# An attention kernel: GpSimd's parts of a product are released one VectorE instruction earlier, and the written order of the work is replaced

## The chip, the cores and the metric

The kernel runs on one core of a Trainium2 chip. The metric is the device time of one execution in microseconds (us); less is better. Times below are medians of several runs, and one execution was taken by the profiler as well.

## What is computed

Grouped-query attention over 8 batches, 8 query heads, 2 key/value heads, 1024 positions and a head size of 64, in float32 in and out:

```
for g in range(n_kv_heads):
    scores = scale * np.matmul(q_group, k_group.transpose(0, 1, 3, 2))
    attn = np.exp(scores - scores_max)
    attn = attn / (np.sum(attn, axis=-1, keepdims=True) + 1e-08)
    output[:, q_start:q_end, :, :] = np.matmul(attn, v_group)
```

## The kernel before

There are 64 jobs, one for each batch and query head. A job has 8 tiles of scores: 128 keys by 1024 queries, in PSUM. So 512 tiles of scores go through the kernel, and each needs an exponential before TensorE can multiply it with the values.

**TensorE** makes a tile with two matmuls (line 760), into one of three PSUM slots `sp`. Later it multiplies the exponentials with the values, 128 queries ("a piece") at a time, into the banks `ops` (line 824). A column of ones in `va` gives the sums of the softmax.

**ScalarE** turns most tiles into exponentials: one activation of 128x1024 from PSUM into `pt` (line 770).

**VectorE** does the rest by arithmetic on the bits of bfloat16, in steps:

- the pass (line 782): a tile from PSUM, scaled and shifted, written as 16-bit integers into `yt`. Two tiles share one buffer, and are called a chain;
- `zh` (line 790): the mantissa bits of `yt` as a number, into `zt`, over 2048 columns, SBUF to SBUF;
- `two` (line 797): the exponent bits of `yt`, into `et`, likewise;
- `mul` (line 806): `zt` times `yt`, SBUF and SBUF to SBUF.

The exponential is the sum of `et` and `zt`. TensorE forms the sum for nothing but more matmuls: it multiplies both with the values. Only the last three jobs add them on VectorE (`add`, line 811). When seven pieces are complete in a bank, VectorE takes the reciprocals of the sums (`rec`, line 889) and scales the outputs (`norm`, line 899), which SyncE's queue stores.

**GpSimd** takes a share of `mul`. The pass, `rec` and `norm` read PSUM; `zh`, `two` and `mul` read and write SBUF alone, and are called SBUF steps here. While VectorE is at a pass (and a `norm` or `rec` beside it), a window opens, and GpSimd multiplies a part of the columns of a chain whose `zh` is done and whose `mul` is still to come (line 738). VectorE's own `mul` is shorter by as much. GpSimd also issues the casting loads of q, k and v (line 518), and a small memset `tick` (line 733) which waits until the buffer of a new chain is free.

**The order** is written out by hand as a string `ORDER`, a letter for each step of TensorE and VectorE: `A` and `a` to `d` make a tile of scores for ScalarE or VectorE, `V` is a few matmuls with values, `W` waits, `p` or `P` is a pass, `r` or `R` a `rec`, `n` a `norm`, a digit is the next SBUF step of one of the open chains. The class `Plan` runs through it with a table of durations (the constants `M_...`, in ns) and makes a list of events with times. The kernel then issues the events by time, and every engine keeps that order. Nothing is decided on the chip.

GpSimd's parts come out of the plan. The function `Plan.gpsimd` is called at a pass, or at the `rec` ahead of it, with the length of the window. It lets a part begin `M_GLEAD` = 160 ns after VectorE has come to the window (or after GpSimd is free), counts `M_GFIX` = 190 ns and `M_GCOL` = 1.88 ns for each column, lets the part end `M_GOVER` = 60 ns behind the window, and makes it as wide as that allows, in steps of 8 columns. VectorE's next SBUF step is counted as held up from the point at which GpSimd ends over `M_GFREE` = 85 ns behind that step's start.

In the kernel, the part is made to wait for the VectorE instruction ahead of its window (`vec`, the last one issued):

```
tc.add_manual_dep(gps.ins, vec.ins.name, Sync, reason="VectorE needs the port before")
```

Of the kernel before, what the change touches and what calls it, by code (L numbers as in the profile page):

```python
# [30 lines left out]
M_D2 = 0.521  # L31
M_D4 = 0.261
M_REC = 115
M_GLEAD = 160
M_GFIX = 190
M_GCOL = 1.88
M_GOVER = 60
M_GLATE = 900
M_GFREE = 85
M_ISSUE = 850  # L40
M_OVER = 5000
NEED = 5150
M_GFREE = 85
M_OVER = 5000
NEED = 5150
M_NORM = 531
# [8 lines left out]
LONG = 6  # L55
GFROM = 2
GTO = 5
GMIN = 96
GREST = 64
GSTEP = 8  # L60
STEPS = (("zh", M_D4), ("two", M_D4), ("mul", M_D2), ("add", M_D2))


ORDER = """
AaApFFFFWWWWFAWWWWWWWWWWWWWWWWWWWWWWWWWWWWaWWWWWWWWWWApEEWWAW0WWWbWWWWApEEWWAW0WWWaWWWWApEEWWA0WWbFF
WAFFpFEAWWW0WWWAAE0W0WWWWWWWWWWWWWWWaRAnWWWWRWWWPWAVVVVVVVVnA0bWWWWApVVVVVVVVA0aWVpAVVVVVAR0bVVA0VVV
pVVVAVVVVnVAb0VVVApVVVAV0VVVVA0bVVRVPVAVVVVVAnbV0AVpVVVVVAVV0VVA0bVVRVPVAVVVVVAnbW0WWAVVpVVVVVVAV0VV
VVA0bWWRWAPVVVVVVVVAnbW0WWAVVpVVVVAVVV0VVVVA0cWWWRWAPVVVVVVVVAnbW0WWAVVVpVVVAVVV0VVVVAR0cWWWAPVVVVVV
VVAnbWW0WWAVVVpVVVVVAVV0VAc0VVVRVPAVVVVAnVA0WbVVVpVVVVAVVV0WVVA0bWWWWARPVVVVVVVVAncWWWA0VVVpVVVAVVVV
0VVA0bVVArPVVVVVVA0WcWWWAPVVVVVVVVAnAV0VVVV0VVVARb0VVVVPVVVAVVVVcnAVpVVVVVAVV0VVAb0VVVVRVAPVVVVVVAnW  # L70
cWWWA0VVVVpVVVVAVVV1VVAc0VARVPVVVVVVAWnWWWbA0VVVVVpVAVVVVVV0VAc0WWWAVpVVVVVVVA0WbWWARVPVVVVVVVAnWWcW
WA1VVVV0VVApVVVVVVVARWnWbWWApVVVVVVVVA0WcWWWApVVVVVVVVVA1cWWWARPVVVVVVVVVVAncWW1WAVVV2VVVVApVVVVVVVV
VA00WcWWAVVRVPVVVVVAVVnVVVA1bWWWWApVVVVVVVVA0cWWRWAPVVVVVVVVAncWW01WWAVVpVVVVVVAWV0VcA1VVVVpVAVVVVAR
0AVVc1VVVPVVVAVVVVnVAc1WWWWAVpVVVVVVVARWW0WcWWAPVVVVVVVVVAnWAV1VVVVVVVV1VcARVPVVVVVVAVnVVVA0cV1VVVVA
pVVVVVAW1WWWcWApVVVVVVVVA0cWWWARVPVVVVVVVAnWWcWWA1VVVVpVVVVAVVVVR0VAc1WWWAVPVVVVVVVAnWWcWA0VVVVVpVVV
AVVVVRV0Ac1WWWAVPVVVVVVVAWnWWWcA0VVVVVpVVVAVVVV2AAV0VVVVVV0VbWWARPVVVVVVVVVVAncWWWA1VVVVpVVVVVAVVVVr
V2VAc2WWWAVPVVVVVVVAnWWWbWA0VpVVVVVVVARWW2WcWWAVPVVVVVVVAnWWbWWA0VVVVpVVVVAVVV0VVAAWWRWWc0VVVVPVVVVA
VVVnVAA1VVVVV1VVVVVA0bVVVVRVPVVVVAVVVVAnc1VVVApVVVVVVVVA1WWbWWApVVVVVVVVVVAR0c1WWWAVVPVVVVVVAVVnVVVV
VA0bVVVpAVVVVVAR1bWWWWAPVVVVVVVVAncWW0WWAVVpVVVVVVAVV0VA1bVRVPVVAVVVVVnAA0VVVVV1VVVVVA0bVVpVAVVVVVVR
A1AVnVVVV1VbWWAipVVVVVVVVA0cWWWARPVVVVVVVVVAnbWWWA1VVVVpVVVVVAVVVV0cA0VVVVApVVVVVVVAR1AVVVnVVVVb1WWA  # L80
VpVVVVVVVVA0WcWAVpVVVVVVVVAR0AWWWbVV0VVVVAPVVVVVVVAncWWARPVVVVVVVAnWWAV1VVVVVV0cWAVpVVVVVVVA1WAWWcRV
nVVVVVpVVAVVVA01cVVpVAVVVVVV0AAWWW0WcVVVRVPVVVVAVVVnVVA1cWWWApVVVVVVVVA1AWWWbR0VVVVPVVVVAVVVnVVA1cWW
WApVVVVVVVVAR0WcWWWAPVVVVVVVVAnAV1VVVVVb0WAVpVVVVVVVARW0WcWWAPVVVVVVVVAnbWWWA1VVV0VVVVVApVVVVVVA0WcW
ARVPVVVVVVVVAnWAV1VVVVVVb0WWAVpVVVVVVVVVARW0WbWWAPVVVVVVVVVVAnAV1VVVVVVb0WAVpVVVVVVVVVARW0WAWWb0VVVV
VVPVVAVVVVVVVnVAb1WWAVpVVVVVVVA0WWbWARVPVVVVVVVAnWWAV1VVVVVV0VVVA1bVVVpVVAVVVVA0WbVRVPVVVAVVVVVAnA1W
VVVVVV1VVcAipVVVVVVVVA0WWbVRAPVVVVVAnVVA1bVV1VVVVApVVVVVVA0WbWWARPVVVVVVVVAnAV1VVVVVb1WAVpVVVVVVVARW
0WaWWAPVVVVVVVVAnbWWWW1WAVVVpVVVVVAVV0VVVA0aWWARPVVVVVVVVVAnAV1VVVVVVVb1AVpVVVVVVVVVARWW0WbWAPVVVVVV
VAVnVVVVVV1VAb1WWWWAVpVVVVVVVVVA0WWbWARVPVVVVVVVVAnWWbWWA1VVVVVpVVVVAVVV1bAVpVVVVAVV0VAr1cVVPVVAVVVV
AnAV1VVVVV0VVbARVpVVVVVVAWnWWWcWA1VVVVVpVVVAVVV0VVA0bWWWApVVVVVVVVAR1AWWWc1VVVVVPVVVAVVVVnVAb0WWWAVp
VVVVVVVARW1WAWWcV1VVVVVPVVAVVVVVnAc0WWWAVpVVVVVVVARWW1WbWAVPVVVVVVVAnWWcWA0VVVVpVVVAVVVV0cAVRpVVAVVV  # L90
VVnVAb1WWWWApVVVVVVVVA0cWWWRWAPVVVVVVVVAnbWW1WWAVVVpVVVVVAVV0VVVARc0WWWAPVVVVVVVVAnbWW1WAVVVpVVVVVVA
VV0VVAA0VVVV1VVVVVVVRc0AVPVVVVVVVAVnVVVA0bVVVApVVVVVVVVAR1AVVVnVVVVVV0VVVVA1aVVVpVAVVVVVVA0bWWWWARPV
VVVVVVVAnbWWW1WAVVV1VVVApVVVVVVVA0WbWWARPVVVVVVVVAnbWWW1WAVVVpVVVVVAVV1VAA0VVV0VVVVVVVVVVARnbVVVVpVA
VVVVVA0b0VVApVVVVVVVVAR0bWWWWAPVVVVVVVVVAnbW0WWAVVpVVVVVVAV0VVAARnVVVVV0VVVVVVVVA1AVVV1VVVVVV0VAAVVV
RVV0VVVVVVVVAnAVVV0VVVVVVVVVVVVVVRAnaWWWApVVVVVVVVVxVA0ArVnVVVVVVV0VA0AVVV0VVVVVLLRnLLLLLWWLFFRFn
"""


# [29 lines left out]
class Plan:  # L128
# [5 lines left out]
    def __init__(self, nj, npt, nct, nyt):  # L134
# [23 lines left out]
        s.tG, s.tB = M_START + 9000, 0  # L158
        s.due = [(NEED * j - 24000, "q", j) for j in [*range(10, nj, 2), nj - 1]]
        for b in range(1, 8):  # L160
            s.due.append((NEED * 8 * b - 16000, "v", (b, 0)))
            if b > 1:
                s.due.append((NEED * 8 * b - 25000, "k", (b, 0)))
        s.due.sort(key=lambda e: e[0])
# [42 lines left out]
    def gpsimd(self, s, t, window):  # L207


        while s.due:  # L210
            x = max(s.tG, s.due[0][0])
            if x + M_ISSUE > t + M_GLEAD:
                if t - s.due[0][0] <= M_OVER:
                    break
                x = max(t, s.tG)
            s.ev.append((x, s.due[0][1], None, s.due[0][2], None))
            s.tG = x + M_ISSUE
            s.due.pop(0)
        at = max(t, s.tG)
        until = t + window + M_GOVER  # L220
        at += M_GLEAD
        for ch in s.chains:
            if not (ch.zend <= at and 1 <= ch.at <= 2 and ch.nsteps == 3):
                continue
            if not GFROM <= ch.pairs[0][0] < self.nj - GTO:
                continue
            w = int((until - at - M_GFIX) / M_GCOL) // GSTEP * GSTEP
            if w < GMIN:
                break
            if ch.cols - w < GREST:  # L230
                w = ch.cols
            if not w:
                continue
            ch.cols -= w
            ch.wins += 1
            s.ev.append((t, "gmul", None, ch.id, (ch.cols, w)))
            s.tB = s.tG = at = at + M_GFIX + w * M_GCOL
            ch.parts += 1
            self.part(s, ch, s.tG + M_SEE + M_GLATE)

    def dve(self, s):
# [60 lines left out]
        else:  # L302
# [7 lines left out]
            if cols:  # L310
                s.ev.append((t, kind, None, ch.id, n, cols))
                end = at + M_FIX + cols * rate
                end += max(0, s.tB - at - M_GFREE)
            if kind == "zh":
# [123 lines left out]
def kernel(  # L438
# [13 lines left out]
    Sync = mybir.DependencyInfo(mybir.DependencyClass.Sync, mybir.DependencyReason.DATA)  # L452
# [216 lines left out]
    for j in range(NJ):  # L669
        b, h = divmod(j, H)  # L670
        at = need[j]
# [28 lines left out]
    def flat(t):  # L700
        return t.bitcast(BF16).rearrange("p i a b -> p (i a b)")
# [10 lines left out]
            elif (j, c) in pt:  # L712
                yield ci, pt[(j, c)][:, par, :]

    vec, gps = None, None
    turns, begun, ended, jobs = [], {}, {}, {}

    def begin(kind, j, gate):
# [4 lines left out]
    for when, kind, x, j, c, *cols in ev:  # L723
# [5 lines left out]
        elif kind == "gmul":  # L729
            lo, w = c  # L730
# [7 lines left out]
            begun[j] = gps = nc.gpsimd.tensor_tensor(  # L738
                out=z, in0=flat(yt[j])[:, lo : lo + w], in1=z, op=ALU.mult
            )  # L740
            tc.add_manual_dep(gps.ins, vec.ins.name, Sync, reason="VectorE needs the port before")
        elif kind == "tk":
            turn_k(*j)
        elif kind == "fv":
# [7 lines left out]
        elif kind == "score":  # L752
            b, h = divmod(j, H)
            t = kt[(b, h // HPG)]
# [21 lines left out]
        elif kind == "dpass":  # L776
            ch, i = j
            where[c] = j
            jobs.setdefault(ch, []).append(c[0])
            if i == 0:  # L780
                yt[ch] = yp.tile([128, CHN, 2, HS], U16, name="yt")
            vec = nc.vector.tensor_scalar(  # L782
                out=yt[ch][:, i, :, :], in0=where_s[c],
                scalar1=EXP_A, scalar2=EXP_B, op0=ALU.mult, op1=ALU.add,
            )
        elif kind == "zh":

            zt[j] = zp.tile([128, CHN, 2, HS], U16, name="zt")
            turns.append(j)
            vec = nc.vector.tensor_scalar(  # L790
                out=zt[j][:, 0:c], in0=yt[j][:, 0:c], scalar1=0x7F, scalar2=0x3F00,
                op0=ALU.bitwise_and, op1=ALU.bitwise_or,
            )
        elif kind == "two":

            et[j] = ep.tile([128, CHN, 2, HS], U16, name="et")
            vec = ins = nc.vector.tensor_scalar(  # L797
                out=et[j][:, 0:c], in0=yt[j][:, 0:c], scalar1=0x7F80, scalar2=None,
                op0=ALU.bitwise_and,
            )  # L800

            while stores and stores[0][0] < when - 10000:
                tc.add_manual_dep(ins.ins, stores.pop(0)[1].ins.name, Sync, reason="old stores")
        elif kind == "mul":
            z = flat(zt[j])[:, 0 : cols[0]]
            vec = nc.vector.tensor_tensor(  # L806
                out=z, in0=flat(yt[j])[:, 0 : cols[0]], in1=z, op=ALU.mult
            )
        elif kind == "add":
            z = zt[j].bitcast(BF16)[:, 0:c]  # L810
            vec = nc.vector.tensor_tensor(
                out=z, in0=et[j].bitcast(BF16)[:, 0:c], in1=z, op=ALU.add
# [59 lines left out]
        elif kind in ("rec", "norm"):  # L872
# [11 lines left out]
            if kind == "rec":  # L884
                rec = rp.tile([128, NPIECE], FP32, name="rec")
                to = rec[:, 0:n]
                if lo >= plan.last:
                    to = to.rearrange("p (b s) -> p b s", b=2)
                vec = nc.vector.reciprocal(out=to, in_=sums)  # L889
            else:  # L890
# [5 lines left out]
                for e, i, m, src in parts:  # L896
                    by = rec[:, i : i + m].unsqueeze(2).to_broadcast([128, m, D])
                    to = ost[:, r + i : r + i + m, :]
                    vec = nc.vector.tensor_tensor(out=to, in0=src, in1=by, op=ALU.mult)  # L899
# [43 lines left out]
```

## Time and profile before

| what | us |
|---|---|
| median of 3 runs (lowest, highest) | 353.49 (353.34, 353.73) |
| the profiled execution | 352.8 |
| its span in the trace | 350.7 |
| ScalarE busy | 343.2 (98%) |
| TensorE matmuls busy | 343.4 (98%) |
| VectorE busy | 341.9 (97%) |
| GpSimd busy | 210.4 (60%) |

The profiled execution took 2.1 us more than its span, which begins with the first instruction and ends with the last. Records of neighbours on an engine overlap by some 0.08 us on VectorE and 0.12 us on ScalarE, so that busy shares near 100% don't tell what is at its limit; the chain of waits does. GpSimd's records are those of line 738 (its parts), 518 (loads issued) and 733 (`tick`).

### The profile page before, as it was taken

To read this page: it belongs to the slowest core of one execution; us is meant where nothing else is said; L and a number is where in the kernel's file an instruction comes from. 1 tells how busy PE (TensorE), PEld (TensorE's weight loads), DVE (VectorE), ACT (ScalarE), POOL (GpSimd) and SP (SyncE) were. 2 spreads that over 40 slices of the span, in tenths; PEclk is the share of its full clock that TensorE was granted. 3 is DMA by queue.
4 is the path that set the end of the run, shared out by engine and by line. 5 is a ranking of instruction groups with operands and counts; after the bars stand their busy time and mean duration, and the time that the engine had idled before them with its cause. 6 is when DMAs were issued, how large, how long until landed. Compare 5 with 4: busy or idle time off the path is not lost.

```text
span 350.7 us, 14208 instructions
## 1 busy us (share of the span) xinstructions
PE 343.4 (98%) x6254; PEld 223.9 (64%) x6254; DVE 341.9 (97%) x518; ACT 343.2 (98%) x374; POOL 210.4 (60%) x248
## 2 busy tenths in 40 slices
PE   8899999999999999999999999999999999999995
PEld 3466666666666666666666666666666666666674
DVE  5999999999999999999999999999999999999995
ACT  6999999999999999999999999999999999999995
POOL 3156667776766766877557566776668766654000
PEclk9999999999999999999999999999999999999999
DMA  7899667686776756596767966967766965564124
GB/s 165 117 154 154 137 128 145 111 151 138 122 137 127 142 105 137 107 177 111 141 105 153 159 143 110 155 122 145 108 122 123 160 158 78 114 131 102 39 63 122
DMA packets 96574, 44.84 MB, mean 128 GB/s; under 512 B 61168, under 2 KB 95344, under 8 KB 95728
## 3 DMA queue, kind: packets, MB, share of 16 engines
q1 hardware_dynamic: 94128, 31.34, 45.3%
q0 software_dynamic: 2096, 12.19, 23.5%
q8 instruction: 49, 0.80, 1.0%
q10 hardware_dynamic: 288, 0.39, 0.4%
q14 instruction: 13, 0.11, 0.1%
HBM read 27.13 MB, written 28.97 MB: 160 GB/s over the span
## 4 chain that ended last, share of the span: by engine, by line
ACT 89%; PE 9%; issue 1%; DVE 0%; DVEq 0%
ACT pt L770 89%; PE ops L824 4%; PE sp L760 3%; PE ops L620 1%; PE sp L864 1%; PE sp L643 0%; DVE ost L899 0%; PE ops L655 0%; PE ops L643 0%; DVEq L938 0%; DVE warm L512 0%; DVE rec L889 0%
## 5 line engine op out<-in xcount | busy, mean ns | idle before, releaser
L770 ACT ACTIVATE pt<-sp 128x1024 bf16<-128x1024 f32 x370 | 340.6, 1039 | 0.2 <-PE sp L760 0.2
L738 POOL TENSOR_TENSOR zt<-yt,zt 128x448 bf16<-128x448 bf16 (+6 forms) x132 | 168.6, 1277 | 99.0 <-DVE et L797 41.3
L824 PE MATMUL ops<-va,pt 128*128 128x65 bf16 x2856 | 175.1, 194 | 0.0
L782 DVE TENSOR_SCALAR yt<-sp 128x1024 uint16<-128x1024 f32 x142 | 171.9, 1210 | 0.9 <-PE sp L760 0.5
L760 PE MATMUL sp<-qt,kt 64*128 64x512 bf16 x1024 | 170.3, 382 | 2.4 <-ACT pt L770 1.6
L824 PEld LDWEIGHTS <-pt 128*128 128x128 bf16 x2856 | 127.3, 97 | 31.5 <-issue 31.5
L824 PE MATMUL ops<-va,zt 128*128 128x65 bf16 x1112 | 128.8, 194 | 0.0
L824 PE MATMUL ops<-va,et 128*128 128x65 bf16 x1080 | 122.3, 194 | 0.0
L824 PEld LDWEIGHTS <-et 128*128 128x128 bf16 x1080 | 84.4, 98 | 20.1 <-issue 20.1
L824 PEld LDWEIGHTS <-zt 128*128 128x128 bf16 x1112 | 88.3, 97 | 11.7 <-issue 11.7
L760 PEld LDWEIGHTS <-kt 64*128 64x128 bf16 x1024 | 49.8, 93 | 54.4 <-issue 32.0
L790 DVE TENSOR_SCALAR zt<-yt 128x2048 uint16<-128x2048 uint16 (+1 forms) x72 | 48.9, 679 | 0.2
L797 DVE TENSOR_SCALAR et<-yt 128x2048 uint16<-128x2048 uint16 (+1 forms) x72 | 48.2, 674 | 0.0
L806 DVE TENSOR_TENSOR zt<-yt,zt 128x872 bf16<-128x872 bf16 (+12 forms) x69 | 45.4, 659 | 0.0
L899 DVE TENSOR_TENSOR ost<-ops,rec 128x448 f32<-128x448 f32 (+2 forms) x73 | 44.4, 608 | 0.3
L518 POOL DMA_DIRECT2D qd<-in_q_dram x33 | 22.0, 668 | 3.6 <-PE sp L760 2.7
L889 DVE RECIPROCAL rec<-ops 128x7 f32<-128x7 f32 (+2 forms) x73 | 14.3, 195 | 0.0
L733 POOL MEMSET tick<- 128x1 bf16 x59 | 11.6, 197 | 0.0
L518 POOL DMA_DIRECT2D kd<-in_k_dram x8 | 5.1, 639 | 5.2 <-PE sp L760 5.2
L620 PE MATMUL ops<-warm 128*128 128x128 bf16 (+1 forms) x22 | 4.5, 345 | 1.2 <-DVE warm L512 1.2
L518 POOL DMA_DIRECT2D vd<-in_v_dram x8 | 5.4, 672 | 0.4 <-PE sp L760 0.4
L620 PEld LDWEIGHTS <-warm 128*128 128x128 bf16 x22 | 1.9, 115 | 3.7 <-issue 2.5
(39 smaller groups left out, 27.0 us busy)
## 6 DMA issues: line engine op xcount, KB each, us to landing
out_dram<-ost SPq DMA_DIRECT2D x63, 256.0 KB, 3.1
qd<-in_q_dram POOLq DMA_DIRECT2D x29, 256.0 KB, 5.0
kt<-kt SPq DMA_DIRECT2D x30, 64.0 KB, 3.8
va<-vd SPq DMA_DIRECT2D x30, 64.0 KB, 4.2
kd<-in_k_dram POOLq DMA_DIRECT2D x7, 256.0 KB, 4.5
vd<-in_v_dram POOLq DMA_DIRECT2D x7, 256.0 KB, 4.9
qt<-qd SPq DMA_TRANSPOSE x63, 4.3
qd<-in_q_dram POOLq DMA_DIRECT2D x5, 128.0 KB, 3.7
```

The source lines that it names most:

```text
L518: return nc.gpsimd.dma_start(out=t.rearrange("(a x) d -> a (x d)", a=128), in_=src.rearrange("(a x) d -> a (x d)", a=128),)
L733: early = nc.gpsimd.memset(tick, 0.0)
L738: begun[j] = gps = nc.gpsimd.tensor_tensor(out=z, in0=flat(yt[j])[:, lo : lo + w], in1=z, op=ALU.mult)
L760: now = nc.tensor.matmul(sps[x][:, half, :], lhsT=t[lo : lo + D, c // NH, ci % NH * 128 : (ci % NH + 1) * 128], rhs=qt[j][lo : lo + D, 0, ...
L770: exps.append(nc.scalar.activation(out=p, in_=where_s[(j, c)], func=AF.Exp, scale=scale))
L782: vec = nc.vector.tensor_scalar(out=yt[ch][:, i, :, :], in0=where_s[c], scalar1=EXP_A, scalar2=EXP_B, op0=ALU.mult, op1=ALU.add,)
L790: vec = nc.vector.tensor_scalar(out=zt[j][:, 0:c], in0=yt[j][:, 0:c], scalar1=0x7F, scalar2=0x3F00, op0=ALU.bitwise_and, op1=ALU.bitwise_or,)
L797: vec = ins = nc.vector.tensor_scalar(out=et[j][:, 0:c], in0=yt[j][:, 0:c], scalar1=0x7F80, scalar2=None, op0=ALU.bitwise_and,)
L806: vec = nc.vector.tensor_tensor(out=z, in0=flat(yt[j])[:, 0 : cols[0]], in1=z, op=ALU.mult)
L824: ended[job] = nc.tensor.matmul(ops[plan.group_of[x] % 2][:, lo : lo + D + 1], lhsT=p[:, qs * 128 : (qs + 1) * 128], rhs=va[(b * G + h // ...
L889: vec = nc.vector.reciprocal(out=to, in_=sums)
L899: vec = nc.vector.tensor_tensor(out=to, in0=src, in1=by, op=ALU.mult)
```

## The change

A part no longer waits for the last SBUF step ahead of its window, but for the VectorE instruction ahead of that step (`gate`). The plan counts a lead of 20 ns in place of 160, but starts no part earlier than 33 ns after the point at which the chain's `zh` counts as done. The least width is 64 columns in place of 96. `ORDER` is replaced as a whole by one made for these constants, so that all engines have a new order. Three constants that stood twice stand once.

```
-M_GLEAD = 160
+M_GLEAD = 20
+M_ZLEAD = 33
...
-GMIN = 96
+GMIN = 64
...
 ORDER = """
-AaApFFFFWWWWFAWWWWWWWWWWWWWWWWWWWWWWWWWWWWaWWWWWWWWWWApEEWWAW0WWWbWWWWApEEWWAW0WWWaWWWWApEEWWA0WWbFF
+AaApFFFWWWWWFAWWWWWWWWWWWWWWWWWWWWWWWWWWWWaWWWWWWWWWWApEEWWEA0bWWWApEFWWWWWAW0WWWaWEpAEWWFA0bFWWWFAF
...
             # in Plan.gpsimd
-            if not (ch.zend <= at and 1 <= ch.at <= 2 and ch.nsteps == 3):
+            if not (ch.zend <= t + 160 and 1 <= ch.at <= 2 and ch.nsteps == 3):
                 continue
+            begin = max(at, ch.zend + M_ZLEAD)
...
-            w = int((until - at - M_GFIX) / M_GCOL) // GSTEP * GSTEP
+            w = int((until - begin - M_GFIX) / M_GCOL) // GSTEP * GSTEP
...
-            s.tB = s.tG = at = at + M_GFIX + w * M_GCOL
+            s.tB = s.tG = at = begin + M_GFIX + w * M_GCOL
...
             # where the part is issued
-            tc.add_manual_dep(gps.ins, vec.ins.name, Sync, reason="VectorE needs the port before")
+            tc.add_manual_dep(gps.ins, gate.ins.name, Sync, reason="the port goes to the step behind it")
...
         # and ahead of each of "zh", "two", "mul" and "add":
+            gate = vec
```

Counted in the order of the built programs:

| | before | after |
|---|---|---|
| activations (ScalarE tiles) | 370 | 369 |
| passes (VectorE tiles) | 142 | 143 |
| `zh` and `two`, each: of 2048 and of 1024 columns | 70 and 2 | 69 and 5 |
| `mul` on VectorE: instructions, columns | 69, 69184 | 68, 60952 |
| `add`: of 2048 and of 1024 columns | 2 and 1 | 1 and 3 |
| GpSimd's parts: instructions, columns | 132, 76224 | 133, 85480 |
| the commonest widths of parts (count) | 448 (69), 792 (27), 728 (25) | 520 (56), 800 (25), 864 (23) |
| matmuls with values in the main stream (line 824) | 5048 | 5056 |
| turns of TensorE between scores and values | 497 | 489 |
| `rec`, `norm` | 74, 74 | 74, 74 |

Of the 133 parts after, 18 wait for nothing that an earlier part had not waited for, and 9 still wait for the `zh` of their own chain, whose data they need. The other 106 are released by the instruction ahead of the last SBUF step, which is a `two` for 50 of them, a `zh` for 31 and a `mul` for 25.

More of the change, by code (lines that the diff above doesn't have):

```diff
@@ L40 @@
 M_ISSUE = 850
-M_OVER = 5000
-NEED = 5150
-M_GFREE = 85
 M_OVER = 5000
@@ L64 @@
 ORDER = """
-AaApFFFFWWWWFAWWWWWWWWWWWWWWWWWWWWWWWWWWWWaWWWWWWWWWWApEEWWAW0WWWbWWWWApEEWWAW0WWWaWWWWApEEWWA0WWbFF
[L66 to L94, printed above, removed]
@@ L95 @@
-RVV0VVVVVVVVAnAVVV0VVVVVVVVVVVVVVRAnaWWWApVVVVVVVVVxVA0ArVnVVVVVVV0VA0AVVV0VVVVVLLRnLLLLLWWLFFRFn
+AaApFFFWWWWWFAWWWWWWWWWWWWWWWWWWWWWWWWWWWWaWWWWWWWWWWApEEWWEA0bWWWApEFWWWWWAW0WWWaWEpAEWWFA0bFWWWFAF
+0FEpAEA0aWWWA0WWWWWWWWWWWWAWrWWnWWWWWWpWWWWAVVVVVVVrA0bVnVVApVVVVVA0WaWWWWApVVVVVVARW0VbWA0VVVVPVVVV
+AVVVnVVA0bWWWApVVVVVVVVAr1AWWWb0VVVVPVVVVAVVVnVVA0bWWWApVVVVVVVVAR0bWWWA0VVVV0VVVVAPVVVVVAWnWWWbWAip
+VVVVVVVVAR1cWWWA0VVVVPVVAVVVVVnVVA0bWVApVVVVVVA0cW0WWAVVV0VVVVVARPVVVVVAnWWWbWAipVVVVVVVVA0cV0VAVRPV
@@ new lines @@
+VVVAVVVnVAb0VVVVpAVVVVA0WbV0VVARVPVVVVAVVnVVVA0cWWWWApVVVVVVVVA0b0WWWAVVpVVVVVAVVRV0cAVPVVVAVVVnVVVA
+0AV0VVVVVRb0WWAVPVVVVVVVVVAnWbWWAipVVVVVVVVVA0AV0VVVVVVVRV0bAVPVVVVVVVVAnWbWWAipVVVVVVVA0WbV0VVARVPV
+VVAVVVnVVA0bVVApVVVVVVVVA0AV0VVVVVV0VbWARVPVVVVVVVVAnWWbWWAipVVVVVVVVVVA0c0WWAV0VVVVVVRVpAVVVVVAnbVi
+VipVAVVVVA1bVVpVAVVVVVAR0c0VVVPAVVVVVAnWbWWWA1VVVVpVVVAVVV0VVA0cVVRVAPVVVVVAnWAV1VVVVVV0AbV0VVVVVARP
+VVVVVVVVAncWWWAipVVVVVVVVVVA1bWWWApVVVVVVVVVVA1cWW0WARVPVVVVVVVVAnAV1VVVVVb0WAVpVVVVVVVAWW0WWWWcAVrp
@@ new lines @@
+VVVVVVAVnVAc1VVVVpVVAVVVVV0Arc0WWWAVPVVVVVVVAnWcWWA1VVVVpVVVVAVVV0VVAR0cWWWAPVVVVVVVVAnWAV0VVVVVVV0V
+VAc0VVVVRAPVVVVVAnWWcWWAipVVVVVVVVA0A0WWWbVV0VVVVVRVPAVVVVVAnWcWWWAipVVVVVVVVA1bWWWApVVVVVVVVA1cWWWR
+WA0PVVVVVVVVAnAV1VVVVVV0AbV0VVVVVVVRAPVVVVVVAnWcVVipAVVVVVVVA0b0WWWAVVpVVVVVVAVVRV0cAVPVVVVVAVVnVVAb
+1VVVVpVVVAVVVVVV0A0bWWWAipVVVVVVVVVAR1AVVVnVVVVV1cAVpVVVVVVAW0WWWbWApVVVVVVVVVAR1cWAPVVVVVVVVVAnbWW0
+WAVpVVVVVVVAWRWW1WcAVPVVVVVAVVnVVVA0cVVpVAVVVVVVVV0AR1cWWWWAPVVVVVVVVVVAncWW0WAVVV1VVVVApVVVVVVVARW0
@@ new lines @@
+WbWWAPVVVVVVVAnWAV1VVVVVV1VcAipVVVVVVVARWW0WcWWA1VVVVVPVVVAVVVnVVAc1WWWAVpVVVVVVVARW2WcWWAVPVVVVVVVA
+nWWcWWA01VVVVpVVVVAVVV0VVAcWWRWAPVVVVVVVVVAncW1WWAVVVpVVVVVVAVV1VVVVA2AVVV2VVVVVVcR0AVPVVVVVVVAnWWcW
+AipVVVVVVVVA0cW1WWAVVRVPVVVVVAVVnVVVA1bWWWApVVVVVVVVA0cRWW1WAVVVPVVVAVVVVnVVVA0AWWWb0VVVVVpVAVVVVVVR
+A0AVVVnVVVVV0cAVpVVVVVVVAW0WWWWcAipVVVVVVVVVARW1WcWWAVPVVVVVVVVVAnWWcWWA0VpVVVVVVAVV0VAc1VVVVRVAPVVV
+VVVVAnbW0WWWAVpVVVVVVVA0WWAWWc1VVVVVRVPVVAVVVVVnAc0WWWApVVVVVVVVA0WcWWWApVVVVVVVVA1cWWWARPVVVVVVVVAn
@@ new lines @@
+AV0V1VVVVVA0cVRVnVVVVApVVVVVVVVA0WcWWApVVVVVVVVVVA0cWWWApVVVVVVVVVVA1cWWWRWApVVVVVVVVVAncWW0WWApVVVV
+VVVVA1AVRV0VVVVVc0AVVVPVVVVAVVVnVVA1cWWWWApVVVVVVVVAR0AWWWc0VVVPVVVAVVVVnVVVA1cWWWApVVVVVVVVAr0cVVPA
+VVVVVAnAV01VVVVVV0AcV1VVVVVVRVPAVVVVVVAnWcViVipVVAVVVVVV0VAc1WWWAVpVVVVVVVVArWnWcWWAVpVVVVVVVA0WWcWA
+pVVVVVVVVA1AWWWc0VVVVRVPVVVAVVVVnVAc0WWWApVVVVVVVVA1cWWWARPVVVVVVVVAnAV2VVVVVV0VVVVVA0b0WWWAVpVVVVVV
+VAW0WWWcAVVRVPVVVVVAVVVVnVAb1VVVVApVVVVVVVAR0cWWWAPVVVVVVVVVVAnbWWW01WAVVVpVVVVAVVVVV0VcARVPVVVVAVVV
@@ new lines @@
+nVVAA0VV1VVVVVVV0VAb1VVVVVVpVVVAVVVVV0VAcWWWWARPVVVVVVVVVAnWAWV1VVVVVVV1VVVVVAR0bVAPVVVVVVVAncWWWAip
+VVVVVVVA0AV0VVVVVRV0bWAPVVVVVVVVAnWcWWWAipVVVVVVVVA1cWWWWApVVVVVVVVAR0b0WWWAVPVVVVVVVAnWWcWWA1VVVVpV
+VVVAVVVVR1VAb0WWWAVPVVVVVVVAnWcWWA1VVVVpVVVVAVVVRc0APVVVVAVVnVVVA1cWWWWApVVVVVVVA0cVRVVPAVVVVVAnAV01
+VVVVVV0VVVVA1cVVpVVVVAVVVVVRV0AcWWAPVVVVVVVVVVAnAV1VVVVVV1VVVVVA0bVVRVPAVVVVVAncWWWWiWiWiAipVVVVVVVV
+A0b0WWWAVpVVVVVVVAW0WWWcAVpVVVVVVVARWnWcWWApVVVVVVVVA1cWWWARPVVVVVVVVAnWAV01VVVV0VVVVA0AVVVVVVra0VnV
@@ L96 @@
+VApVVVVVVVAWW0WWWbWAVpVVVVVVVVA0WWA1WVV0VVVV0VbARVPVVVVVVAVVnVVVVA2VV0VVAA0V1VVVVVVRV0bWAVPVVVxVVAVn
+VVVA0AVVVVVVVVV1VVVA0WAVVVVVVVRV0VVVVnVVVVVA0AV0VVVVVVVVVRVnVaApVxVVVVVVVVVA0WAWW0WAV0VVVVVVV0VVVVVV
+VARnAVVVVVVVVVLRLnLLLLLLFFRFn
 """
@@ L713, in terms @@
                 yield ci, pt[(j, c)][:, par, :]
-    vec, gps = None, None
+    vec, gps, gate = None, None, None
     turns, begun, ended, jobs = [], {}, {}, {}
@@ L794 @@
         elif kind == "two":
+            gate = vec
             et[j] = ep.tile([128, CHN, 2, HS], U16, name="et")
@@ L804 @@
         elif kind == "mul":
+            gate = vec
             z = flat(zt[j])[:, 0 : cols[0]]
@@ L809 @@
         elif kind == "add":
+            gate = vec
             z = zt[j].bitcast(BF16)[:, 0:c]
```

## The prediction

> **What bounds the kernel now.** First the page: its span, and the shares of the chain that ended last.
>
> ```profile
> span 350.7 us, 14208 instructions
> ACT pt L770 89%; PE ops L824 4%; PE sp L760 3%; PE ops L620 1%; PE sp L864 1%; PE sp L643 0%; DVE ost L899 0%; PE ops L655 0%; PE ops L643 0%; DVEq L938 0%; DVE warm L512 0%; DVE rec L889 0%
> ```
>
> The chain runs along the activations: from 5.82 us in the timeline to 346.43 us they take 340.6 us for 370, or 0.921 us each, with a median of 0.914 us from start to start; all their stalls come to 2.4 us. So time goes with the number of activations, as long as VectorE and TensorE keep the slots moving. Then the groups by line.
>
> ```profile
> L770 ACT ACTIVATE pt<-sp 128x1024 bf16<-128x1024 f32 x370 | 340.6, 1039 | 0.2 <-PE sp L760 0.2
> L738 POOL TENSOR_TENSOR zt<-yt,zt 128x448 bf16<-128x448 bf16 (+6 forms) x132 | 168.6, 1277 | 99.0 <-DVE et L797 41.3
> L782 DVE TENSOR_SCALAR yt<-sp 128x1024 uint16<-128x1024 f32 x142 | 171.9, 1210 | 0.9 <-PE sp L760 0.5
> ```
>
> GpSimd idles 99.0 us ahead of its parts, for SBUF steps; VectorE hardly idles at all. Behind 8 us, its gaps (start minus the neighbour's end, plus the usual overlap of 0.08 us) come to 5.0 us, 1.0 of it at the very end. Both it and ScalarE are at their limits.
>
> Third, the timeline of VectorE, where a window opens and closes, and then GpSimd's.
>
> ```profile
> 98.95 1.17 DVE L782 TENSOR_SCALAR yt<-sp 128x1024 uint16<-128x1024 f32 x1
> 100.57 0.73 DVE L790 TENSOR_SCALAR zt<-yt 128x2048 uint16<-128x2048 uint16 x1
> ...
> 144.52 1.22 DVE L782 TENSOR_SCALAR yt<-sp 128x1024 uint16<-128x1024 f32 x1
> 145.65 0.98 DVE L806 TENSOR_TENSOR zt<-yt,zt 128x1600 bf16<-128x1600 bf16 x1
> 146.67 0.65 DVE L797 TENSOR_SCALAR et<-yt 128x2048 uint16<-128x2048 uint16 x1
> 147.24 1.21 DVE L782 TENSOR_SCALAR yt<-sp 128x1024 uint16<-128x1024 f32 x1
> 148.90 0.68 DVE L790 TENSOR_SCALAR zt<-yt 128x2048 uint16<-128x2048 uint16 x1
> 149.50 0.68 DVE L797 TENSOR_SCALAR et<-yt 128x2048 uint16<-128x2048 uint16 x1
> ```
> ```profile
> 98.99 1.71 POOL L738 TENSOR_TENSOR zt<-yt,zt 128x808 bf16<-128x808 bf16 x1 [0.80 <-DVE et L797]
> ...
> 144.68 1.03 POOL L738 TENSOR_TENSOR zt<-yt,zt 128x448 bf16<-128x448 bf16 x1 [0.58 <-DVE zt L806]
> 146.68 0.67 POOL L733 MEMSET tick<- 128x1 bf16 x1
> 147.40 1.41 POOL L738 TENSOR_TENSOR zt<-yt,zt 128x648 bf16<-128x648 bf16 x1
> 148.76 0.91 POOL L518 DMA_DIRECT2D vd<-in_v_dram  x1
> 149.67 0.55 POOL L733 MEMSET tick<- 128x1 bf16 x1
> ```
>
> Four things are read here. (1) A released part starts 0.16 us behind the pass (144.68 against 144.52), which is 0.08 us behind the end of the step's record; the median over 127 parts is 0.081 us. A part of w columns then takes 190 + 1.88w ns (448: 1.03 us). (2) It ends 0.06 us into the next SBUF step (145.71 against 145.65), and the step doesn't suffer. Where parts end 0.093 to 0.117 us into a step, fifteen of sixteen steps keep their length; at 0.139 us (98.99 + 1.71 against 100.57) the step takes 0.73 in place of 0.68. So a part may end some 35 to 55 ns later than planned for nothing, and each ns more costs VectorE one. (3) A GpSimd instruction that meets an SBUF step in progress is held, and the step isn't: the memset at 146.68, otherwise 0.1 us, ends 0.03 us behind the `two`; the load at 148.76 ends 0.09 us behind the `zh`, and the memset of 149.67 0.04 us behind the `two`. In all, held memsets end 27 to 37 ns behind the step, held loads 94 to 98. (4) The memset of 146.68 came 8 ns behind its step and lost. So the step has the port at once, and GpSimd gets it between two steps.
>
> **The change, part by part.** *The earlier release.* The gate is the instruction just ahead of the SBUF step. By (1) the part would start 0.16 us behind the step's own start; by (4) that is some 0.15 us too late to take the port first. So 106 parts will sit held through the step and go on when it ends. No row shows a held part; its price is what is left of its fixed 190 ns. The memset is nearest: of its 0.1 us some 35 ns were left, so about 60 were hidden. With 60 hidden, 130 ns are left, and the part ends 130 + 1.88w ns behind the step's record. That is 210 + 1.88w from the window's start, just what the plan counts (20 + 190). Bounds: 35 left (all hidden but what the memset shows), or 95 + 190 = 285 (woken like a load, and nothing hidden). I take 130; under it nothing is gained, as the order is fixed.
>
> [...]
>
> *Wider parts.* 140 ns less lead is 74 columns at 1.88 ns, and the common parts grow by 72. GpSimd gets 9256 columns: 17.4 us and one start, on an engine that is busy 60%; its DMA issues (49) and memsets stand behind parts in its queue as before, and the loads are due some 16 to 25 us ahead, and SyncE's issues move with the events that they follow, so the cost is nothing. If that cover went, TensorE would wait for a load, and its rows show no such wait.
>
> *VectorE.* From the groups by shape, less 0.08 us of overlap: a pass is 1.13 us; `zh` 0.607 (2048) and 0.342 (1024), `two` 0.601 and 0.339; `add` 1.134 and 0.612; `mul` 0.524 ns a column (2048: 1207 ns, 808: 557) and 0.054 a start. So: one pass +1.13; `zh` −0.607 + 3 × 0.342 = +0.42; `two` +0.42; `add` −1.134 + 2 × 0.612 = +0.09; `mul` −8232 × 0.000524 − 0.054 = −4.37. The sum is −2.31 us.
>
> *ScalarE.* One activation fewer: −0.92 us on the chain (−0.91 without stalls).
>
> *TensorE.* Eight matmuls with values more, at 0.93 / 27 = 0.034 us in the chain's rows: +0.28 us. Eight turns fewer: ahead of values TensorE's weight loads wait 63.3 us in 242 gaps, 0.26 each, so −2.1 us at most. It waits for slots besides; I take nothing, between −0.92 (more couldn't show while ScalarE is the path) and +0.28.
>
> *Start and end.* From the last activation to the end of the span are 4.3 us: products, `rec`, `norm`, store. The written order has two waits fewer among the last products and is otherwise the same there; I leave the end as it is.
>
> *The sum.* 352.8 − 0.92 = 351.9 us for the profiled execution, whose median stood at 353.49: 353.49 − 0.92 = 352.57, so **352.6 us**. VectorE is relieved by 2.31 and must keep up with 0.92, so 1.4 us are left to cover late parts. Twelve memsets are held by a step now; a part behind one starts late by up to 50 ns, mostly within the spare of (2).
>
> **The rivals.** *1, no change:* nothing of the 190 ns is hidden. A part has 190 left, ends 60 ns late, 0.12 us into the next step, and costs 5 to 27 ns there: × 106 = 0.5 to 2.9 us on VectorE. Less the cover of 1.4 us that is from nothing to +1.5, so 352.6 to 354.1 us. It also stands for a saving eaten by stalls of the new order, which are 2.4 us on ScalarE now. For it: the plain start of a part has no row that splits it. Against it: the memset hides 60 of 95.
>
> *2, slower:* the held part is woken like a load and starts from nothing. With 285 left it ends 155 ns late, 0.215 us into the step, and costs 100 to 122 ns × 106 = 10.6 to 12.9 us on VectorE, less 1.4 of cover and at most 4.0 of VectorE's gaps: 5.2 to 11.5 us, so 357.8 to 364.1 us. It decides from 165 to 185 ns left. From 0.16 us into the step on, GpSimd's next part would be free to go too, and each step that loses the port to one waits a whole part, 1.2 to 1.8 us. For it: loads take 95. Against it: parts are computed like memsets, not issued like loads.
>
> *3, the release isn't earlier in truth:* a data wait on the step itself. The built program has it for 9 parts alone. Then 106 parts end 140 ns late, 0.2 us into a step: the price of rival 2, as good as excluded.
>
> *4, better:* the new order also saves half of ScalarE's 2.4 us of stalls: 351.4 us.
>
> **How the numbers follow.** A measurement of this kernel can tell about 0.2% (0.7 us) from no change, so faster is below 352.8 us and slower above 354.2. Forecast 0.47, rival 4 0.05 (both faster, 0.52). Rival 1 0.31, of which 0.05 end above 354.2. Rival 2 0.15 and rival 3 0.02. So faster 0.52, same 0.26, slower 0.22. The range runs from 351.6 (most of rival 4 left out) to 355.0, which takes in rival 1 with VectorE's loss whole on the path, and leaves out rivals 2 and 3: some 0.2.
>
> **What would show it.** Right: 369 activations at 0.92 us; held parts of 520 columns in records of about 1.6 us (from 0.16 us into a 0.6 us step to 130 + 978 ns behind its record), and GpSimd's idle time ahead of parts well below 99 us; parts ending 0.06 us into the next step; `zh` and `two` still 0.68 us. Wrong: parts ending beyond 0.12 us into the step and `zh`, `two` or `mul` longer by as much (rivals 1 and 2); a step of 1.5 us or more (a lost port); more gaps ahead of activations with the steps unchanged (the order).

## The result

| | before | after |
|---|---|---|
| median of 15 runs each (lowest to highest), us | 353.42 (352.81 to 353.87) | 352.61 (352.22 to 353.24) |
| ratio of the times, 95% interval | | 0.9979 (0.9971 to 0.9987) |

The change saves 0.2%, some 0.7 to 0.8 us, and the interval leaves out no change. Measured once more, in the run e8_after_again below, the ratio was 0.9981.

A single profile would have misled here. Of the changed kernel it shows the slowest of its 15 runs (353.24 us), and of the kernel before one at the low end (352.8 us), so that the span grew by 0.4 us although the medians fell. First the page after: its span, its chain by engine and by line, and the groups of the activations, of GpSimd's parts and of the passes.

```profile
span 351.1 us, 14216 instructions
...
PE 74%; ACT 19%; DVE 5%; DMA 1%; issue 0%; DVEq 0%
PE ops L828 40%; PE sp L760 33%; ACT pt L770 19%; DVE yt L782 3%; DMA q<-in_q_dram 1%; DVE ost L903 1%; PE sp L868 1%; DVE et L799 0%; DVE zt L791 0%; DVE zt L809 0%; PE sp L643 0%; PE ops L655 0%; DVE rec L893 0%; ACT q L632 0%; DVEq L942 0%
...
L770 ACT ACTIVATE pt<-sp 128x1024 bf16<-128x1024 f32 x369 | 339.9, 1038 | 0.7 <-PE sp L760 0.6
L738 POOL TENSOR_TENSOR zt<-yt,zt 128x520 bf16<-128x520 bf16 (+10 forms) x133 | 224.1, 1689 | 44.4 <-DVE zt L791 14.5
L782 DVE TENSOR_SCALAR yt<-sp 128x1024 uint16<-128x1024 f32 x143 | 173.1, 1211 | 1.1 <-PE sp L760 0.8
```

GpSimd's idle time ahead of parts fell from 99.0 to 44.4 us. Its busy time rose by 55.5 us, of which 17.4 are more columns and the rest is waiting inside the records of held parts. The chain left ScalarE for TensorE: ScalarE's share fell from 89% to 19%, and TensorE has 74%. That isn't a slower TensorE: its matmuls take as long as before (194 ns in the mean with values, 382 and 383 ns with scores). The chain is followed back from whichever came last at each step, and here several engines are within fractions of a microsecond of each other.

So the span is best taken apart: the start up to the first activation, the stretch of the activations, and the tail. The numbers are from the timelines, in us.

| trace | start | stretch | tail |
|---|---|---|---|
| before; two executions more (e10, e11) | 5.82; 5.98, 5.91 | 340.6; 340.6, 341.0 | 4.3; 4.6, 4.3 |
| after; again (e8) | 6.66; 6.20 | 340.0; 339.9 | 4.5; 4.3 |

The stretch, which the change is about, is 0.6 us shorter against the first trace, and 0.8 between the means. That the profiled span grew all the same comes from a start 0.84 us later and a tail 0.24 us longer; the start is taken up at the end.

Now VectorE and GpSimd after the change, at a `zh` (106.54) and a `two` (108.68) which hold a part each. What an SBUF step and a part can't have at the same time is called the port. VectorE's timeline, then GpSimd's (start, duration, engine, line, and idle time before in brackets).

```profile
106.54 0.68 DVE L791 TENSOR_SCALAR zt<-yt 128x2048 uint16<-128x2048 uint16 x1
107.14 1.22 DVE L782 TENSOR_SCALAR yt<-sp 128x1024 uint16<-128x1024 f32 x1
108.28 0.37 DVE L809 TENSOR_TENSOR zt<-yt,zt 128x424 bf16<-128x424 bf16 x1
108.56 0.20 DVE L893 RECIPROCAL rec<-ops 128x7 f32<-128x7 f32 x1
108.68 0.64 DVE L799 TENSOR_SCALAR et<-yt 128x2048 uint16<-128x2048 uint16 x1
109.24 1.22 DVE L782 TENSOR_SCALAR yt<-sp 128x1024 uint16<-128x1024 f32 x1
...
110.90 0.68 DVE L791 TENSOR_SCALAR zt<-yt 128x2048 uint16<-128x2048 uint16 x1
```
```profile
106.71 1.54 POOL L738 TENSOR_TENSOR zt<-yt,zt 128x520 bf16<-128x520 bf16 x1 [0.19 <-DVE ost L903]
...
108.74 0.61 POOL L733 MEMSET tick<- 128x1 bf16 x1
108.84 2.04 POOL L738 TENSOR_TENSOR zt<-yt,zt 128x800 bf16<-128x800 bf16 x1
```

The part of 106.71 begins 0.17 us into the `zh`, released by the `norm` ahead of it, and waits in its own record. It ends at 108.25, which is 1.02 us behind the end of the `zh`: 0.98 for 520 columns, and 0.05 of the fixed 0.19. The `zh` is as long as ever. The next SBUF step starts at 108.28, so the part is out of the way 0.03 us ahead of it, where a part before the change ended 0.06 us into it.

Over the trace, 106 parts are held so: 31 by a `zh`, 50 by a `two`, 25 by a `mul`. Behind the step's record they need 1.88 ns a column and another 52, 53 and 57 ns (medians; the lowest is 45). The plan counts 130.

### The profile page after: what moved, and what is told of

Its sections match the earlier page's. It is cut to its first block, busy times and chain, and to the rows that moved or that the text cites. A ratio compares the mean times of both kernels' runs of the same rounds, so it can differ in the third digit from the quotient of the medians.

```text
span 351.1 us, 14216 instructions
## 1 busy us (share of the span) xinstructions
PE 343.9 (98%) x6262; PEld 225.7 (64%) x6262; DVE 340.4 (97%) x523; ACT 342.5 (98%) x373; POOL 262.9 (75%) x249
## 4 chain that ended last, share of the span: by engine, by line
PE 74%; ACT 19%; DVE 5%; DMA 1%; issue 0%; DVEq 0%
PE ops L828 40%; PE sp L760 33%; ACT pt L770 19%; DVE yt L782 3%; DMA q<-in_q_dram 1%; DVE ost L903 1%; PE sp L868 1%; DVE et L799 0%; DVE zt L791 0%; DVE zt L809 0%; PE sp L643 0%; PE ops L655 0%; DVE rec L893 0%; ACT q L632 0%; DVEq L942 0%
## 5 line engine op out<-in xcount | busy, mean ns | idle before, releaser
L770 ACT ACTIVATE pt<-sp 128x1024 bf16<-128x1024 f32 x369 | 339.9, 1038 | 0.7 <-PE sp L760 0.6
L738 POOL TENSOR_TENSOR zt<-yt,zt 128x520 bf16<-128x520 bf16 (+10 forms) x133 | 224.1, 1689 | 44.4 <-DVE zt L791 14.5
L828 PEld LDWEIGHTS <-pt 128*128 128x128 bf16 x2848 | 126.0, 97 | 29.3 <-issue 29.3
L760 PEld LDWEIGHTS <-kt 64*128 64x128 bf16 x1024 | 51.0, 93 | 54.4 <-issue 31.7
L903 DVE TENSOR_TENSOR ost<-ops,rec 128x448 f32<-128x448 f32 (+2 forms) x73 | 44.4, 608 | 0.2
L809 DVE TENSOR_TENSOR zt<-yt,zt 128x728 bf16<-128x728 bf16 (+15 forms) x68 | 41.3, 607 | 0.0
```

Source lines behind the costliest of these rows:

```text
L738: begun[j] = gps = nc.gpsimd.tensor_tensor(out=z, in0=flat(yt[j])[:, lo : lo + w], in1=z, op=ALU.mult)
L760: now = nc.tensor.matmul(sps[x][:, half, :], lhsT=t[lo : lo + D, c // NH, ci % NH * 128 : (ci % NH + 1) * 128], rhs=qt[j][lo : lo + D, 0, ...
L770: exps.append(nc.scalar.activation(out=p, in_=where_s[(j, c)], func=AF.Exp, scale=scale))
L809: vec = nc.vector.tensor_tensor(out=z, in0=flat(yt[j])[:, 0 : cols[0]], in1=z, op=ALU.mult)
L828: ended[job] = nc.tensor.matmul(ops[plan.group_of[x] % 2][:, lo : lo + D + 1], lhsT=p[:, qs * 128 : (qs + 1) * 128], rhs=va[(b * G + h // ...
```

## The experiments

**e1_gate_old_plan: the release alone.** The kernel before, with `gate` in place of `vec`; its order, widths and constants stay.

```
+            gate = vec        # ahead of each SBUF step
-            tc.add_manual_dep(gps.ins, vec.ins.name, ...)
+            tc.add_manual_dep(gps.ins, gate.ins.name, ...)
```

> The kernel before with the new gate alone: its order, its widths and its constants stay. Theory (the earlier release pays only through wider parts and the activation that they save): held parts end 50 ns + 1.88 ns a column behind the record of the step, as after the change, so about 0.16 us ahead of the next SBUF step in place of 0.06 us into it; nobody waits for that, and the time stays at 353.4 us, within 0.2%. Rival A (the earlier release itself saves time): 352.6 us or less. Rival B (the held part harms the step that holds it, and the new order only covers it): zh and two longer than 0.69 us, 354.2 us or more.

Measured: 353.01 us, ratio 0.9995 (0.9986 to 1.0004). Its groups show the parts held, and the activations as before:

```profile
L770 ACT ACTIVATE pt<-sp 128x1024 bf16<-128x1024 f32 x370 | 340.6, 1038 | 0.3 <-PE sp L760 0.3
L738 POOL TENSOR_TENSOR zt<-yt,zt 128x448 bf16<-128x448 bf16 (+6 forms) x132 | 209.9, 1591 | 61.5 <-DVE zt L791 22.3
```

114 parts are held, with 51 to 57 ns left behind the step (medians), and end 0.16 us ahead of the next SBUF step. `zh` and `two` have the length that they had (678 and 675 ns in the mean, 679 and 674 before). So holding a part costs the step nothing, and an earlier end of a part that nobody waits for is worth nothing that this measurement can tell. Rivals A and B fall.

**e2_old_wait_new_plan: the new order and widths, the old wait.**

```
-            tc.add_manual_dep(gps.ins, gate.ins.name, ...)
+            tc.add_manual_dep(gps.ins, vec.ins.name, ...)
```

> The kernel after the change with the old wait: its order and its wider parts stay, but a part waits for the last SBUF step again. Theory: parts start 0.16 us into the window and end 190 + 1.88w later, 140 ns later than planned, so 0.20 us into the next SBUF step, which is then 0.09 to 0.11 us longer; 106 times that is 9 to 12 us on VectorE, of which 1.4 us are covered by its relief and up to 4 us by its gaps: 357 to 363 us. Rival (the order alone made the gain, the release is not needed): 352.6 us within 0.2%.

Measured: 355.54 us, ratio 1.0067 (1.0053 to 1.0080). It is slower, as the theory had it, and 2.9 us above the changed kernel; the size was expected too large. VectorE's timeline and GpSimd's at the same place as above:

```profile
107.19 1.21 DVE L782 TENSOR_SCALAR yt<-sp 128x1024 uint16<-128x1024 f32 x1
108.32 0.43 DVE L809 TENSOR_TENSOR zt<-yt,zt 128x424 bf16<-128x424 bf16 x1
```
```profile
107.35 1.16 POOL L738 TENSOR_TENSOR zt<-yt,zt 128x520 bf16<-128x520 bf16 x1 [0.58 <-DVE zt L791]
```

The part starts 0.16 us into the window and ends at 108.51, 0.19 us into the `mul`, which takes 0.43 us in place of 0.37. That is the overlap that the theory gave. But over more than forty such steps, with overlaps from 0.196 to 0.274 us, the length added is the overlap less 0.13 us (196 ns: 64; 245: 114). Three steps grew by more, one of them by 139 ns at 236; in all three a memset or a load stands right behind the part in GpSimd's queue. The spare behind a step's start is thus 0.13 us, not 0.095 to 0.115. And only 72 steps are over 20 ns longer, 5.5 us in all, where 106 were counted. So with these widths the earlier release is needed: without it, the wider parts cost more than they bring. Whether an order made anew for the old wait could have saved an activation too, no run tests.

**e3_wider and e9_wider_again: parts wider by 40 columns.** The plan's lead goes from 20 to -55 ns, which fills most of the 78 ns by which it overrates a held part. `ORDER` is rewritten to fit the new plan, mostly with letters that only let it idle, so that TensorE and ScalarE keep their order. VectorE keeps its own too, but for four `mul` that GpSimd takes over whole (64 in place of 68); GpSimd has 136 parts in place of 133, and its loads and memsets stand elsewhere among them.

```
-M_GLEAD = 20
+M_GLEAD = -55
...
```

> The kernel after the change with a planned lead of -55 ns in place of 20: each part about 40 columns wider, filling the 80 ns by which parts end earlier than planned; the order of each engine stays, and so do the 369 activations. Theory (time goes with the activations; VectorE's relief alone is not on the path): parts end some 0.05 us into the next SBUF step, no step is longer, VectorE's mul gets about 1.7 us shorter, and the time is that of the change, 352.6 us within 0.2%. Rival (VectorE sets the pace now): 351.0 to 351.8 us.

> The kernel with parts wider by 40 columns again (lead -55 ns), beside e8_after_again. Theory (time goes with the activations): the ratio to before is that of e8_after_again within 0.1%. Rival (VectorE's relief pays, since activations wait less): lower by more than 0.1%, as the first measurement (0.9972 against 0.9979) hinted.

Measured: 352.23 us, ratio 0.9972 (0.9962 to 0.9983), and again 352.03 us, ratio 0.9968 (0.9955 to 0.9980). Beside the second one the changed kernel was run again:

> The kernel after the change once more, on the chip and beside the runs of before that e9_wider_again shares: 0.9979 of before, within its interval of 0.9971 to 0.9987. If the first activation again starts later than at 5.9 us, the new order's start is slower; if it starts at 5.8 to 5.9 us, the start differs from execution to execution and not by the change.

That gave 352.60 us, ratio 0.9981 (0.9972 to 0.9990). The common parts have 560 and 840 columns, no step suffers (one over 20 ns in the first trace), and the records of VectorE's work, less their overlap, sum to 334.4 us in place of 336.9 (the second pair: 335.9 and 337.9). The stretch of the activations is 339.8 us in both. So with 2.0 to 2.5 us less on VectorE the medians are 0.4 and 0.6 us lower. The intervals of the ratios overlap, but beside e8 all five runs of the wide version (351.99 to 352.13 us) lie below all eleven of the changed kernel (352.14 to 352.97), so the wide version is the faster one. Not all of that is VectorE's relief: some 0.2 us lie outside the span, where every run of the wide version spends 1.83 to 1.93 us and every run of the changed kernel 2.06 to 2.21. Why, the record doesn't show. The medians of the spans are 0.15 and 0.3 us shorter, and the stretch 0.1 to 0.2.

**e4_two_up: the gate one instruction further up.**

```
-            gate = vec
+            gate = seen[-2]   # the VectorE instruction ahead of vec
```

> The kernel after the change with the gate one instruction further up: a part waits for the second instruction ahead of the last SBUF step. Theory (whoever comes first has the port to the end of its instruction): where a norm, a pass or another SBUF step lies ahead of the last SBUF step (29, 23 and 34 of 106 parts), the part takes the port first, and the step waits for what is left of it: about 0.9, 0.3 and 1.3 us each, 77 us in all on VectorE if nothing is won back, and at least 15 us on the time; SBUF steps of 1.2 us and more appear. Rival (the step goes first though the part has come before it, so the place of the gate doesn't matter): 352.6 us within 0.2%.

Measured: 417.35 us, ratio 1.1812 (1.1778 to 1.1846). VectorE's timeline and GpSimd's at the first of the long `two` steps between 92 and 98 us (here line 802 is `two`, 812 `mul`, 785 the pass, 741 the parts):

```profile
92.31 1.20 DVE L785 TENSOR_SCALAR yt<-sp 128x1024 uint16<-128x1024 f32 x1
93.44 0.52 DVE L812 TENSOR_TENSOR zt<-yt,zt 128x728 bf16<-128x728 bf16 x1
93.89 2.31 DVE L802 TENSOR_SCALAR et<-yt 128x2048 uint16<-128x2048 uint16 x1
96.12 0.19 DVE L896 RECIPROCAL rec<-ops 128x7 f32<-128x7 f32 x1
```
```profile
93.60 2.05 POOL L741 TENSOR_TENSOR zt<-yt,zt 128x864 bf16<-128x864 bf16 x1 [1.75 <-DVE yt L785]
```

The part is released by the pass and is held through the `mul`. When the `mul` ends, the `two` has already started by its record (93.89), but the port goes to the part, and the `two` stands until 95.65 and takes 2.31 us in place of 0.68. 68 steps are longer, by 66.3 us in all; the estimate was 77. The place of the gate is exact to one instruction: one lower costs 2.9 us (e2), one higher 64.7.

**e5_four_act: what an activation costs.**

```
             exps.append(nc.scalar.activation(out=p, ...))
+            if len(exps) in (75, 150, 225, 300):
+                nc.scalar.activation(out=p, ...)
```

> The kernel after the change with four activations more: the 75th, 150th, 225th and 300th of the main loop are issued twice, with the same result. Theory (ScalarE's activations set the time): each costs its whole 0.914 us, 3.7 us in all, so 356.3 us (355.6 to 356.5). Rival (TensorE or VectorE sets it, and ScalarE has room): 352.6 to 354.2 us.

Measured: 356.58 us, ratio 1.0094 (1.0079 to 1.0109). That is 4.0 us above the changed kernel, or 1.0 us for each activation, though the chain in the changed kernel's trace runs mostly along TensorE. It lies just above the range of the theory (356.5) and far above the rival's: an activation more costs at least its whole time.

**e6_eight_two and e7_eight_two_gate: what VectorE's time costs.**

```
             vec = ins = nc.vector.tensor_scalar(out=et[j][:, 0:c], ...)
+            if j in (8, 16, 24, 32, 40, 48, 56, 64):
+                gate = vec    # in e7 alone
+                vec = nc.vector.tensor_scalar(out=et[j][:, 0:c], ...)
```

> The kernel after the change with eight more SBUF steps on VectorE: the step two of every eighth chain is issued twice, with the same result, 0.60 us each, 4.8 us in all. Theory (VectorE was relieved by more than the saved activation, and its gaps of 6.5 us in the trace are room): at least 1.4 us and at most all but 0.5 of it are covered, so 352.8 to 356.0 us, about 354 us. Rival A (VectorE sets the time as ScalarE does): 357.0 us or more. Rival B (VectorE has room for all of it): within 0.2% of 352.6 us.

Measured: 368.04 us, ratio 1.0426 (1.0396 to 1.0457), 15.4 us more for 4.8 us of work. All three expectations missed, and the cause lay in the edit: the gate was left two steps up. The groups by shape show what became of the repeated step (line 804) beside the plain one:

```profile
L804 DVE TENSOR_SCALAR et<-yt 128x2048 uint16<-128x2048 uint16 x8 | 13.1, 1642 | 0.3
L799 DVE TENSOR_SCALAR et<-yt 128x2048 uint16<-128x2048 uint16 x69 | 46.7, 680 | 0.0
```

Seven of the eight took 1.54 to 2.19 us: e4's loss, unasked for, in back-to-back SBUF steps. With the gate in its place:

> The eight more two steps of e6_eight_two, with the gate set at the repeated step as at every other one, so that a part is held through the repeated step and can't take the port ahead of it. Theory: e6 took 15 us because in seven of eight places a part, free two steps up, had the port between the two steps, and the repeated step took 1.5 to 2.2 us; without that the eight cost 4.8 us on VectorE, of which the gaps cover some: 353.2 to 357.0 us, no step over 0.75 us. Rival (any work more on VectorE is paid several times over, since the order is fixed): 360 us or more.

Measured: 357.71 us, ratio 1.0130 (1.0116 to 1.0144), and the repeated steps take 694 ns in the mean (of the others, one takes 0.87 us, behind a load, as it does in the changed kernel). 5.1 us more for 4.9 us of work (eight records less their overlap). It is just above the range expected and far below the rival's 360: VectorE's work, added in lumps of 0.6 us, goes into the time whole. No cover by gaps can be seen.

**e10_before_look and e11_before_look: the start.** The kernel before, unchanged.

> The kernel before, one profiled execution more, for its start alone. Theory (the start differs from execution to execution and has nothing to do with the change): the first activation starts anywhere from 5.8 to 6.7 us, late where TensorE's 128-column matmuls ahead of it follow each other in 107 ns in place of 56. Rival (the new order starts later): at 5.8 to 5.9 us, as in the two traces with the old order.

> The same once more: a second sample of the start of the kernel before. Theory: anywhere from 5.8 to 6.7 us; rival: 5.8 to 5.9 us again, which would make four of four.

Measured: 353.24 and 353.26 us, one run each; the first activation starts at 5.98 and 5.91 us. Both are far from the latest start of 6.66 us, and e10 has the matmuls in 107 ns all the same, so the theory's reason for a late start doesn't hold as it stands. Whether the new order starts later is left open; see the last section.

## Why the prediction was right

**Held parts, right in kind, mis-sized.** The parts are held and the step isn't, as rows (3) and (4) had it: not one of 106 took the port first, for steps of all three kinds. The term that failed is "130 left". It is 52 behind a `zh`, 53 behind a `two` and 57 behind a `mul` in the median, nearer to the lower bound of 35 than to 130. So parts with a plain window end some 0.02 us ahead of the next step and not 0.06 us into it. Nothing came of it for the time, as the prediction said of any value under 130; but some 40 columns a part were left unused. Row (3) was worded too widely: of the 59 memsets of before, 29 ran whole inside a `mul`, in 0.09 to 0.12 us, and were not held.

**The spare, too small.** "35 to 55 ns later than planned for nothing" rested on one row, the step at 100.57 us, and that row was misread. Right behind that part, GpSimd had a memset (100.65). In e10 and e11, the same kernel, the same part again ends 0.14 us into the same step. In e10 the memset runs in 0.10 us as before, and the step takes 0.73; in e11 the step holds the memset (0.65 us) and takes 0.69. The memset of before, then the part, the memset and the step of e11:

```profile
100.65 0.10 POOL L733 MEMSET tick<- 128x1 bf16 x1
```
```profile
99.47 1.71 POOL L738 TENSOR_TENSOR zt<-yt,zt 128x808 bf16<-128x808 bf16 x1 [0.71 <-DVE et L797]
101.13 0.65 POOL L733 MEMSET tick<- 128x1 bf16 x1
```
```profile
101.04 0.69 DVE L790 TENSOR_SCALAR zt<-yt 128x2048 uint16<-128x2048 uint16 x1
```

So the part itself cost that step about 0.01 us, and the memset the rest. e2 has over forty rows of longer overlaps, and they say 0.13 us into the step, so 70 ns. By them rival 1, with parts ending at 0.12 us, would have cost nothing at all, and rival 2 no more than 83 ns a part.

**Rivals 1 to 3 fell.** A part that starts from nothing when released would have 190 ns left, one woken like a load 285. Of 106 values two are 138 and 143, and no other is above 64. The page "SBUF — State Buffer" of the Trainium skill (A bandwidth-pool intuition that's wrong) measured "blocked until DVE-end + ~115 ns" (DVE is VectorE) for a DMA issued from GpSimd. That is the case of the held loads (94 to 98 ns in the traces), and the parts don't follow it. Its rule in Who interferes with whom, that issue order decides who blocks, is what e4 shows at its price, and so is its sentence that a VectorE instruction with two SBUF inputs contends with GpSimd's reads: behind `mul` 25 parts were held like the others.

**One activation fewer, right.** −0.92 us was forecast, −0.7 to −0.8 measured, and e5 gives 1.0 us for each one added. In the traces, the stretch lost 0.6 to 0.8 us: between the first two, an activation went from 0.9205 to 0.9213 us, which would be 0.3 us of new stalls over 369 of them; but three traces with the old order alone run from 0.9204 to 0.9215, so this can't be told from chance. Rival 4, fewer stalls, fell. That the forecast of 352.57 us came within 0.04 of the measured 352.61 is partly luck: it started from a median 0.07 too high, and its saving was 0.1 to 0.2 too large. (The median from start to start is 0.916 us in the records, not 0.914; nothing rests on that.)

**The cover, wrong.** The prediction let VectorE's relief of 2.31 us leave 1.4 us to cover late parts, and let up to 4.0 us of its gaps cover more under rival 2. e7 shows no cover for work that comes in lumps: 5.1 us for 4.9. In e2 the many small delays, 5.5 us, cost 2.9, so a part is covered there. What the relief bought, as the plan has it, was one tile more on VectorE, 143 in place of 142, and with it the activation; that it couldn't have been had otherwise is argued, not shown. In the other direction, e3 and e9 take 2.0 to 2.5 us off VectorE, and the span gains 0.15 to 0.3. So VectorE and ScalarE are at their limit together: work added on either is paid in full, and relief of VectorE alone brings little. For TensorE no run tests it.

**VectorE's sum, about right.** −2.31 us was worked out. VectorE's records less their overlap came to 339.0, 339.4 and 339.3 us in the three traces of the kernel before, and to 336.9 and 337.9 in the two of the changed one: −1.8 between the means, with up to 1.0 us between traces of one kernel.

## What to carry to other kernels

Here a wait on the instruction whose end was wanted cost GpSimd 0.08 us and a part's whole fixed 0.19 us behind that end; with a wait on the instruction ahead of it, some 0.05 us were left, since the hardware itself kept the order. It is safe only where the instruction to be protected has the shared resource before the released one can ask for it: here by 0.16 us in the median and 0.04 in four of 106 cases, and one instruction further up the same release cost 18%. The release by itself brought nothing that could be told (e1): the gain came where the plan turned the won time into one instruction fewer on an engine at its limit.

## What had not been expected of the hardware

**The port between back-to-back steps.** A held GpSimd instruction gets the port when the step that holds it ends, even where VectorE's next SBUF step has already started by its record. Row (4) had the port go to GpSimd between two steps, but not the price. Under e4 and e6 such steps took 1.5 us and more. The rows of before showed it only for short memsets and loads, which cost the next step nothing that one could see; in the changed kernel one `two`, behind a load between two such steps (at 303.00 us), takes 0.87 us.

**The start.** In some executions TensorE's first matmuls of 128 columns (line 643), ahead of the first activation, follow each other in 107 ns, in others in 56. TensorE's timeline of before, then of after:

```profile
4.27 0.40 PE L643 MATMUL sp<-ident,q 128*128 128x128 bf16 x4
```
```profile
4.47 0.61 PE L643 MATMUL sp<-ident,q 128*128 128x128 bf16 x4 [0.22 <-ACT q L632]
```

With the q load landing 0.2 us later besides, the first activation starts at 6.66 us in place of 5.82. The page's row of the granted clock has 9 in every slice of both, so it doesn't show this. The first few matmuls don't decide it: with the old order, e10 has 106 to 107 ns there too, and e1 once, and they start at 5.98 and 5.87 us, for their spacing soon falls to 56. In the five traces that start at 6.20 us or later it stays at 106 to 109 through the matmuls of line 655, the next ones, which turn k. With the old order four starts lay between 5.82 and 5.98 us; with the new order, in all its variants, nine lay between 5.95 and 6.66. The instructions ahead of the first activation are the same in both. If all thirteen were drawn from one lot, so lopsided an order would come up in 4 of 715 draws; yet nothing in the traces says how the order could reach that far forward. Whether the new order starts later stays open; the medians hold the start already, and a start earlier by 0.3 us would be worth nearly half of what the change brought.
